# A two-block transformer kernel: latent queries and keys split where they are transposed, a second accumulator bank in the last eight heads, separate banks for the second pair of gates

## The chip, the cores and the metric

The kernel runs on one core of a Trainium2 chip. The metric is the device time of one execution in microseconds (us). Beside the time of each run there is one profiled execution, whose trace tells when each engine did what: PE (TensorE, matmuls; its weight loads are shown apart as PEld), DVE (VectorE), ACT (ScalarE), POOL (GpSimd) and SP (SyncE, which here only issues DMAs).

## The reference, cut to what matters

The input, 1024 tokens of width 1024, goes through two blocks. The first (a mixer of four branches and a gated feed-forward part) is not touched by the change. The second is a hybrid attention layer:

```python
q_a, k_a, v_a, z_a, c_q, c_kv, k_rope, z_b = split(rmsnorm(x) @ w_in)
o_a = dilated_window_attention(rmsnorm(q_a), rmsnorm(k_a), v_a, rel_bias)      # 8 heads of 64
q = rmsnorm(c_q) @ w_uq;  kv = rmsnorm(c_kv) @ w_ukv                          # latent: 8 heads
q_nope, q_rope, k_nope, v = ...            # 64 + 32 wide; norms, then rope on the 32
o_b = softmax(mask((q_nope @ k_nope.T + q_rope @ k_rope.T) * 96 ** -0.5)) @ v
out = x + concat([o_a * silu(z_a), o_b * silu(z_b)]) @ w_out
```

So heads 0 to 7 are windowed heads, and heads 8 to 15 latent heads with queries and keys 96 wide. The gates z_a and z_b are eight blocks ("pairs") of 128 columns.

## The kernel before, in words

Every fp32 matmul is made of matmuls on fp32r operands: a number is split into a high part `hi` (a cast) and a low part `lo` (the number less `hi`), and hi x hi, hi x lo and lo x hi are added up. The helper `split` (lines 99 to 101) does this with a cast on ACT and a subtraction on DVE, or on POOL where it is told so.

The matmul accumulators are eight banks of 128 x 512 fp32: `ip` and `tp` two each, `lt` two, `iq` and `ho` one each. `bank(name)` takes the next free one of a name.

The second block runs in these stages (us from the start of the span):

- About 1760 to 1985: the projections. `compressed`, `latent`, `windowed` and `values` make products of 128 tokens with weights, and their vector work. `latent_out` (line 1600) calls `heads_out` (line 1522) for queries and keys of 128 tokens, and that twice each: PE transposes four heads into the bank `ho`, ACT scales them into a buffer `st` (two of them), and a DMA from ACT's queue stores it in DRAM (`mq`, `mk`, fp32, rows of 512 bytes). There are 8 x 2 x 2 = 32 such calls. `windowed_out` (line 1615) already stores both parts for heads 0 to 7: ACT writes `st`, DVE writes `sl` from the same bank, and two DMAs go out.
- About 1985 to 2015: the gates. `gate_pair` (line 1482) runs 48 matmuls into two banks, then ACT (tanh, line 1498) and DVE (line 1499) empty each. Pair 0 and pair 1 are made here, pairs 2 to 7 (`gates2`) are woven into heads 0 to 7 as filling.
- About 2015 to 2340: the heads. `head_steps` weaves the scores of head h with the value products of head h - 1. A score is two (windowed) or three (latent) matmuls into `lt` or `ho`; DVE adds the mask and takes the minimum (line 1779), ACT takes the exponential (line 1781). The value products (`pv_steps`) go over 12 key blocks, in two groups: 8 blocks for the second half of the queries, then 4 for the first. Per block PE transposes up to four pieces of the probabilities into a bank (line 350), ACT and DVE split that into `pth` and `ptl`, and two matmuls (lines 334 and 335) add to the accumulator `po`. After each group `evict` (line 1801) empties `po`: a copy on ACT (line 1805), a sum on DVE (line 1806); after the second, POOL multiplies with gate and scale (lines 1808 and 1809), and SP stores the result in `mixed`.
- `Head.load` (line 1734) loads a head's queries and keys. For a latent head it loads fp32 `raw` buffers (two) for queries and for keys from `mq` and `mk`, and splits them with a cast on ACT and a subtraction on POOL, 96 x 1024 each. `qh`, `kh`, `kl` and `ql` have two buffers each.
- Beside the latent heads the weights of the output product (`out_weight`, split with POOL) and the first four blocks of `mixed` (`mr`, split with POOL into `mh`, `ml`) are made ready. From about 2320 on the value products of head 15 and the output product follow.

The order on each engine is set by the scheduler of the tile framework, from the program's order and its own estimates; each engine then runs its list in order, and a DMA queue issues in order. So an instruction that waits holds all behind it on its engine.

The lines that decide which bank the heads use:

```python
turns = {"s": ("lt", "lt", "ho"), "pt": ("tp", "tp")}      # line 1721; "pt" are the transposes
banks_ = (lambda: bank("iq"), lambda: next_bank("pt"))     # line 1762; the accumulator is iq
turns["pt"] = ("tp", "tp", "ip", "ip")                     # line 1860, ahead of heads 8 to 15
```

Of the kernel before, what the change touches and what calls it, by code (L numbers as in the profile page):

```python
# [8 lines left out]
F32 = mybir.dt.float32  # L9
F32R = mybir.dt.float32r  # L10
# [55 lines left out]
def kernel(ctx: ExitStack, tc: tile.TileContext, A: dict, out: bass.AP, stop=None):  # L66
# [8 lines left out]
    def f(x):  # L75
        return x.bitcast(F32)
# [1387 lines left out]

    aq_d = dram.tile([2, 512, T], F32, name="aq")
    ak_d = dram.tile([2, 512, T], F32, name="ak")
    mq_d = dram.tile([8, 96, T], F32, name="mq")
    mk_d = dram.tile([8, 96, T], F32, name="mk")
    vt_d = dram.tile([T, 16, 2, 64], F32, name="v2t")
    z_d = dram.tile([1024, T], F32, name="z2")  # L1470
    rd_d = dram.tile([16, T], F32, name="rd")
# [13 lines left out]
    def gate_pair(p, chunks, ps, out):  # L1485

        for half in range(2):
            wh, wl = chunks(0)
            for k in range(4):
                n = 4 * half + k  # L1490
                for w, x, last in ((wh, hh, 0), (wh, hl, 0), (wl, hh, 1)):
                    for j in range(2):
                        PE.matmul(ps[j], w[:, k, :], x[j][:, n, :], start=(n == 0 and w is wh and x is hh),  # L1493
                                  stop=(n == 7 and bool(last)))
                yield
        for j in range(2):
            zt = out()
            S.activation(zt, ps[j], AF.Tanh, scale=0.5)
            V.scalar_tensor_tensor(zt, zt, 1.0, ps[j], op0=ALU.add, op1=ALU.mult)  # L1499
            nc.sync.dma_start(z_d[p * 128:(p + 1) * 128, j * 512:(j + 1) * 512], zt)  # L1500
        yield
# [20 lines left out]
    def heads_out(src, width, dst, t, gain):  # L1522

        for q in range(2):
            pt = quad("ho")[0:width]
            for i in range(4):
                PE.transpose(pt[:, i, :], src[:, 4 * q + i, :], ident)
            st = f(ibw.tile([width, 4, 128], F32R, name="st", bufs=2))
            S.activation(st, pt, AF.Copy, scale=gain)
            S.dma_start(dst[4 * q:4 * q + 4, :, t * 128:(t + 1) * 128].rearrange("h d c -> d h c"), st)  # L1530

    def compressed(t):

# [146 lines left out]
    for p in range(2):  # L1680
        c_ = [gate_weights(p, half, lambda: ibl.tile([128, 512], F32, name="wr", bufs=2).rearrange("p (k c) -> p k c", k=4),
                           lambda: slot(p).rearrange("p (k c) -> p k c", k=4)) for half in range(2)]
        fill.append(gate_pair(p, c_.pop, [bank("ip") for _ in range(2)], lambda: gate_tile()))
        for _ in range(8):
            next(fill[p])
        if p == 0:
            gate_tile = lambda: f(ibw.tile([128, 4, 128], F32R, name="st", bufs=2)).rearrange("p a b -> p (a b)")
            next(fill[p])
# [29 lines left out]
            for _ in range(ZP):  # L1718
                yield

    turns = {"s": ("lt", "lt", "ho"), "pt": ("tp", "tp")}
    turn = {"s": 0, "pt": 0}

    def next_bank(what):
        turn[what] += 1
# [2 lines left out]
    class Head:  # L1728
# [6 lines left out]
        def load(self):  # L1735

            h = self.h
            n = 96 if self.lat else 128
            qh, kh, kl = [at.tile([n, T], F32R, name=name, bufs=2) for name in ("qh", "kh", "kl")]
            if self.lat:  # L1740
                if h == 8:
                    cm_table()
                self.mask = cm[0]
                ql = at.tile([n, T], F32R, name="ql", bufs=2)
                for hi, lo, src in ((qh, ql, mq_d), (kh, kl, mk_d)):
                    raw = at.tile([n, T], F32, name="raw", bufs=2)
                    nc.sync.dma_start(raw, src[h - 8])
                    split(hi, lo, raw, G)
                self.passes = ((qh, kh), (qh, kl), (ql, kh))
            else:  # L1750
                for x, src, ee in ((qh, aq_d, (0, 1)), (kh, ak_d, (0, 0)), (kl, ak_d, (1, 1))):
                    for i, e in enumerate(ee):
                        nc.sync.dma_start(f(x[64 * i:64 * i + 64, :]), src[e, h * 64:(h + 1) * 64, :])
                self.passes = ((qh, kh), (qh, kl))
                self.mask = at.tile([128, T], F32, name="bias", bufs=2)
                nc.sync.dma_start(self.mask, bass.AP(tensor=u_d.tensor, offset=u_d.offset + h * NU, ap=[[1, 128], [1, T]]))

        def values(self):
            h = self.h
            v2 = at.tile([128, 8, 128], F32R, name="v2", bufs=2)  # L1760
            nc.sync.dma_start(f(v2), vt_d[:, h].rearrange("(k p) e d -> p k (e d)", p=128))
            banks_ = (lambda: bank("iq"), lambda: next_bank("pt"))
            self.pv = pv_steps(at, *banks_, v2, self.P, [(1, 0, lambda po: self.evict(po, 1)), (0, 4, lambda po: self.evict(po, 0))],
                               NP_, LAG)
            self.pv.insert(SCL, self.scales)
# [91 lines left out]
    for _ in g2:  # L1857
        pass
    sth.close()
    turns["pt"] = ("tp", "tp", "ip", "ip")  # L1860
    stf = ExitStack()
    fo = stf.enter_context(tc.tile_pool(name="fo", bufs=1, side="right", reuse_waits="tile"))
    for h in range(NG, 16):
# [23 lines left out]
                yield  # L1887

    turns["pt"] = ("tp", "tp")
    braid(weave_steps(heads[15].pv, []), first_products(), FR)  # L1890
    sta.close()
    with tc.tile_pool(name="fp", bufs=1, reuse_waits="tile") as fp:
# [115 lines left out]
```

## Time and profile before

| | |
|---|---|
| median of 3 runs | 2426.95 us (2423.92 to 2432.35) |
| the profiled execution's own time | 2424.3 us |
| its span, first to last instruction | 2422.6 us |
| mean granted clock of TensorE | 0.989 of 2.4 GHz |
| busy: PE, DVE, ACT, POOL | 2322.5, 1467.4, 1067.3, 583.3 us |
| bytes moved by DMA | 309.08 MB |

A stage's table tells for each engine how long it was busy in that stretch; a list of waits tells which engine stood idle until which instruction of another engine ended. The difference between the span and the time, 1.7 us, is what lies around the first and the last instruction.

### The profile page before, as it was taken

To read this page: it belongs to the slowest core of one execution; us is meant where nothing else is said; L and a number is where in the kernel's file an instruction comes from. 1 tells how busy PE (TensorE), PEld (TensorE's weight loads), DVE (VectorE), ACT (ScalarE), POOL (GpSimd) and SP (SyncE) were. 2 spreads that over 40 slices of the span, in tenths; PEclk is the share of its full clock that TensorE was granted. 3 is DMA by queue.
4 is the path that set the end of the run, shared out by engine and by line. 5 is a ranking of instruction groups with operands and counts; after the bars stand their busy time and mean duration, and the time that the engine had idled before them with its cause. 6 is when DMAs were issued, how large, how long until landed. Compare 5 with 4: busy or idle time off the path is not lost.

```text
span 2422.6 us, 31192 instructions
## 1 busy us (share of the span) xinstructions
PE 2322.5 (96%) x11330; PEld 1883.0 (78%) x11330; DVE 1467.4 (61%) x2357; ACT 1067.3 (44%) x1973; POOL 583.3 (24%) x582
## 2 busy tenths in 40 slices
PE   6999899999999999998999997999999999999999
PEld 5887676778777887877788886888798777787787
DVE  4245753578455534579888885556756525678842
ACT  4344433222443323444444342446556525669840
POOL 0122310113223111036555552000023100126510
PEclk9999999999999999999999998999999999999999
DMA  4332115454333258412222224734523647766433
GB/s 153 96 100 83 45 60 165 156 170 138 104 95 105 94 163 240 153 36 79 88 87 81 87 79 152 238 101 150 166 87 109 172 140 206 196 174 186 120 115 134
DMA packets 280442, 309.08 MB, mean 128 GB/s; under 512 B 14928, under 2 KB 209120, under 8 KB 280288
## 3 DMA queue, kind: packets, MB, share of 16 engines
q1 hardware_dynamic: 241296, 266.26, 36.2%
q10 hardware_dynamic: 38848, 40.31, 5.2%
q8 instruction: 89, 1.46, 0.3%
q14 instruction: 65, 0.53, 0.1%
q0 software_dynamic: 144, 0.52, 0.1%
HBM read 217.80 MB, written 89.23 MB: 127 GB/s over the span
## 4 chain that ended last, share of the span: by engine, by line
PE 45%; DMA 5%; DVE 4%; ACT 3%; issue 2%; POOL 1%; SPq 0%; POOLq 0%; ACTq 0%; DVEq 0%
PE ac L1171 11%; PE ip L1171 4%; PE ip L1493 3%; PE tp L350 1%; PE ip L1382 1%; PE ip L1383 1%; PE ip L1384 1%; PE iq L334 1%; PE lt L1777 1%; PE iq L335 1%; DMA wr<-in_w_in_dram 1%; PE ip L1441 1%; PE ip L1043 1%; PE ip L1439 1%; PE ip L1440 1%
## 5 line engine op out<-in xcount | busy, mean ns | idle before, releaser
L123 PE MATMUL mm<-hh,whi 128*128 128x512 f32 x896 | 304.6, 411 | 1.6 <-ACT hh L100 0.9
L123 PE MATMUL mm<-hl,whi 128*128 128x512 f32 x896 | 290.1, 395 | 0.0
L123 PE MATMUL mm<-hh,wlo 128*128 128x512 f32 x896 | 288.4, 393 | 1.3 <-DVE wlo L115 1.3
L100 ACT CAST whi<-wraw 128x1024 fp32r<-128x1024 f32 (+1 forms) x117 | 99.8, 853 | 262.7 <-PE mm L123 197.7
L123 PEld LDWEIGHTS mm<-hh,wlo 128*128 128x128 f32 x896 | 168.6, 189 | 38.8 <-DVE wlo L115 1.9
L123 PEld LDWEIGHTS mm<-hl,whi 128*128 128x128 f32 x896 | 168.1, 189 | 36.0 <-DVE hl L101 0.4
L101 DVE TENSOR_TENSOR wlo<-wraw,whi 128x1024 fp32r<-128x1024 f32 (+1 forms) x117 | 118.2, 1013 | 120.4 <-ACT whi L100 114.6
L123 PEld LDWEIGHTS mm<-hh,whi 128*128 128x128 f32 x896 | 158.9, 190 | 37.7 <-issue 7.1
L167 POOL TENSOR_TENSOR rs<-rs,negh 128x1 f32<-128x1 f32 x32 | 19.5, 612 | 381.1 <-DVE rs L166 381.1
L101 DVE TENSOR_TENSOR gl<-s,gh 128x512 fp32r<-128x512 f32 x88 | 60.7, 690 | 80.3 <-ACT gh L100 77.9
L1781 ACT ACTIVATE p<-p,mn 128x640 f32<-128x640 f32 (+7 forms) x128 | 99.5, 778 | 12.4 <-DVE mn L1779 12.1
L926 POOL TENSOR_TENSOR acc<-acc,pacc 128x1024 f32<-128x1024 f32 x20 | 50.7, 2536 | 199.8 <-DVE acc L921 144.6
L100 ACT CAST uhi<-s 128x1024 fp32r<-128x1024 f32 x42 | 44.1, 1053 | 122.9 <-PE ip L1171 87.6
L101 DVE TENSOR_TENSOR ptl<-tp,pth 128x512 fp32r<-128x512 f32 (+3 forms) x144 | 78.0, 555 | 31.8 <-ACT pth L100 30.6
L100 ACT CAST gh<-s 128x512 fp32r<-128x512 f32 x88 | 54.6, 621 | 94.3 <-PE tp L1440 35.6
L101 DVE TENSOR_TENSOR ulo<-s,uhi 128x1024 fp32r<-128x1024 f32 x42 | 88.0, 2097 | 4.9 <-ACT uhi L100 4.9
L100 ACT CAST pth<-tp 128x512 fp32r<-128x512 f32 (+3 forms) x144 | 66.9, 477 | 43.4 <-PE tp L350 41.3
L1253 POOL TENSOR_TENSOR cv<-th,cv 128x1024 f32<-128x1024 f32 x22 | 53.6, 2434 | 128.6 <-issue 90.2
L334 PE MATMUL iq<-pth,v 128*128 128x512 f32 x192 | 71.7, 375 | 7.8 <-DVE t L1806 4.1
L350 PE MATMUL tp<-cv,p 128*128 128x128 f32 x432 | 71.8, 277 | 1.6 <-DVE ptl L101 1.4
L1808 POOL TENSOR_TENSOR zz<-zz,rdb 128x512 f32<-128x512 f32 x16 | 20.6, 1290 | 216.0 <-DMA qh<-aq 128.2
L1493 PE MATMUL ip<-h3h,zh 128*128 128x512 f32 x192 | 65.6, 409 | 3.7 <-DVE zt L1499 3.7
(591 smaller groups left out, 6437.1 us busy)
## 6 DMA issues: line engine op xcount, KB each, us to landing
wraw<-in_w_in_dram SPq DMA_DIRECT2D x60, 512.0 KB, 4.1
wraw<-in_w_up_dram SPq DMA_DIRECT2D x44, 512.0 KB, 3.9
wr<-in_w_down_dram SPq DMA_DIRECT2D x88, 256.0 KB, 2.9
merged<-acc SPq DMA_DIRECT2D x28, 512.0 KB, 2.9
s<-gg SPq DMA_DIRECT2D x44, 256.0 KB, 4.5
gg<-cv SPq DMA_DIRECT2D x21, 512.0 KB, 2.6
pacc<-merged SPq DMA_DIRECT2D x20, 512.0 KB, 4.1
x<-x ACTq DMA_DIRECT2D x16, 512.0 KB, 2.7
```

The lines of the kernel that those rows point to most:

```text
L100: S.copy(hi, src)
L101: (eng or V).tensor_tensor(lo, src, f(hi), op=ALU.subtract)
L123: PE.matmul(ps[:, c0 + j * 512:c0 + (j + 1) * 512], w[:, k, :], x[j][:, k, :], start=(k == 0 and w is wh and x is xh), stop=(k == nkt - 1 ...
L334: PE.matmul(po[-1][:, w], vh[:, k, :], ph_[:, w], start=(k == 0), stop=False)
L335: PE.matmul(po[-1][:, w], vh[:, k, :], pl_[:, w], start=False, stop=(k == nk - 1))
L350: PE.transpose(pt[:, i * 128:(i + 1) * 128], P[p0 + i][:, k * 128:(k + 1) * 128], ident)
L926: G.tensor_tensor(ac, ac, pa, op=ALU.add)
L1043: PE.matmul(po, ml[:, k, :], W[c][k][0], start=False, stop=(k == NK - 1))
L1171: PE.matmul(acc, a[:, k, :], b[:, k, :], start=(start and k + n == 0), stop=(k == 3 and n == 2), skip_group_check=True)
L1253: G.tensor_tensor(b, self.th, b, op=ALU.mult)
L1493: PE.matmul(ps[j], w[:, k, :], x[j][:, n, :], start=(n == 0 and w is wh and x is hh), stop=(n == 7 and bool(last)))
L1781: S.activation(pr_[:, :L], pr_[:, :L], AF.Exp, scale=-1.0, bias=mn[:, c:c + 1], accum_out=self.den[:, i:i + 1])
```

## The change

1. `heads_out` makes both parts of the latent queries and keys right at the transposes: ACT writes `hi` into `st`, DVE writes `lo` into `sl` from the same bank, and both are stored; `mq` and `mk` get a leading dimension of 2. `Head.load` then loads four tiles, and neither casts nor subtracts. The buffers `raw` are gone.
2. In heads 8 to 15 the accumulator takes turns between `iq` and one of the two `ip` banks, and the transposes rotate over three names in place of four.
3. Gate pair 1 uses `iq` and one `tp` bank; pairs 0 and 2 go on using the two `ip` banks.

```diff
-    mq_d = dram.tile([8, 96, T], F32, name="mq")
-    mk_d = dram.tile([8, 96, T], F32, name="mk")
+    mq_d = dram.tile([2, 8, 96, T], F32, name="mq")
+    mk_d = dram.tile([2, 8, 96, T], F32, name="mk")
...
             pt = quad("ho")[0:width]
             for i in range(4):
                 PE.transpose(pt[:, i, :], src[:, 4 * q + i, :], ident)
-            st = f(ibw.tile([width, 4, 128], F32R, name="st", bufs=2))
-            S.activation(st, pt, AF.Copy, scale=gain)
-            S.dma_start(dst[4 * q:4 * q + 4, :, t * 128:(t + 1) * 128].rearrange("h d c -> d h c"), st)
+            hi = ibw.tile([width, 4, 128], F32R, name="st", bufs=2)
+            lo = ibw.tile([width, 4, 128], F32R, name="sl", bufs=SL)
+            S.activation(hi, pt, AF.Copy, scale=gain)
+            V.scalar_tensor_tensor(lo, pt, gain, f(hi), op0=ALU.mult, op1=ALU.subtract)
+            for e, st in enumerate((hi, lo)):
+                S.dma_start(dst[e, 4 * q:4 * q + 4, :, t * 128:(t + 1) * 128].rearrange("h d c -> d h c"), f(st))
...
-        fill.append(gate_pair(p, c_.pop, [bank("ip") for _ in range(2)], lambda: gate_tile()))
+        fill.append(gate_pair(p, c_.pop, [bank(n) for n in (("ip", "ip"), ("iq", "tp"))[p]], lambda: gate_tile()))
...
-    turns = {"s": ("lt", "lt", "ho"), "pt": ("tp", "tp")}
-    turn = {"s": 0, "pt": 0}
+    turns = {"s": ("lt", "lt", "ho"), "pt": ("tp", "tp"), "po": ("iq",)}
+    turn = {"s": 0, "pt": 0, "po": 0}
...
-                for hi, lo, src in ((qh, ql, mq_d), (kh, kl, mk_d)):
-                    raw = at.tile([n, T], F32, name="raw", bufs=2)
-                    nc.sync.dma_start(raw, src[h - 8])
-                    split(hi, lo, raw, G)
+                for x, src, e in ((qh, mq_d, 0), (kh, mk_d, 0), (kl, mk_d, 1), (ql, mq_d, 1)):
+                    nc.sync.dma_start(f(x), src[e, h - 8])
...
-            banks_ = (lambda: bank("iq"), lambda: next_bank("pt"))
+            banks_ = (lambda: next_bank("po"), lambda: next_bank("pt"))
...
     sth.close()
-    turns["pt"] = ("tp", "tp", "ip", "ip")
+    turns["pt"] = ("tp", "tp", "ip")
+    turns["po"] = ("iq", "ip")
...
     turns["pt"] = ("tp", "tp")
+    turns["po"] = ("iq",)
     braid(weave_steps(heads[15].pv, []), first_products(), FR)
```

The scheduler makes a new order of it. Three places show what moved. Line numbers of the changed kernel are up to 3 higher than those before (the transposes of `windowed_out`, L1618, become L1621; the scores, L1777, become L1778).

The first is PE's list where the latent queries and keys of the later tokens are transposed (`ho<-cv,qq` and `ho<-cv,ko`; `ip` is a projection's bank, `h3h` and `h3l` the parts of the tokens). Before:

```order
L1527 MATMUL ho<-cv,qq 96x128 x4
L1384 MATMUL ip<-s_15266,h3l_11304 128x512
L1382 MATMUL ip<-s_15272,h3h_11302 128x512
L1383 MATMUL ip<-s_15273,h3h_11302 128x512
L1384 MATMUL ip<-s_15272,h3l_11304 128x512
L1382 MATMUL ip<-s_15278,h3h_11302 128x512
L1383 MATMUL ip<-s_15279,h3h_11302 128x512
L1527 MATMUL ho<-cv,ko 96x128 x4
L1384 MATMUL ip<-s_15278,h3l_11304 128x512
```

And after the change:

```order
L1384 MATMUL ip<-s_15344,h3l_11304 128x512
L1527 MATMUL ho<-cv,ko 96x128 x4
L1527 MATMUL ho<-cv,qq 96x128 x4
L1621 MATMUL tp<-cv,an 128x128 x4
L1382 MATMUL ip<-s_15302,h3h_11302 128x512
L1383 MATMUL ip<-s_15303,h3h_11302 128x512
L1384 MATMUL ip<-s_15302,h3l_11304 128x512
L1382 MATMUL ip<-s_15308,h3h_11302 128x512
L1527 MATMUL ho<-cv,qq 96x128 x4
```

Two sets of transposes into `ho` now follow each other with nothing between. A second such pair (`qq`, then `ko`) stands some 55 rows further on, and 26 rows behind that one three sets of `tp<-cv,an` in a row; most other sets stand further apart than before.

The second place is PE's list in a latent head, at the end of its first group of value products. Before:

```order
L334 MATMUL iq<-pth,v_18987 128x128
L335 MATMUL iq<-ptl,v_18987 128x128
L350 MATMUL tp<-cv,p_18999 128x128
L350 MATMUL tp<-cv,p_19017 128x128
L350 MATMUL tp<-cv,p_19033 128x128
L350 MATMUL ip<-cv,p_19017 128x128
L350 MATMUL ip<-cv,p_19033 128x128
L1777 MATMUL lt<-kh,qh 128x256
L1777 MATMUL lt<-kl,qh 128x256
L1777 MATMUL lt<-kh,ql 128x256
```

And after:

```order
L334 MATMUL ip<-pth,v_19067 128x128
L335 MATMUL ip<-ptl,v_19067 128x128
L350 MATMUL tp<-cv,p_19079 128x128
L350 MATMUL tp<-cv,p_19097 128x128
L350 MATMUL tp<-cv,p_19113 128x128
L334 MATMUL iq<-pth,v_19067 128x512
L335 MATMUL iq<-ptl,v_19067 128x512
L350 MATMUL tp<-cv,p_19097 128x128
```

The second group's first products now stand three transposes behind the first group's last, in the other bank; before they stood 22 rows further on, in the same bank.

The third place is SP's list of DMA issues, in one latent head (`raw`, or `qh`, `kh`, `kl`, `ql`, are loads for a later head; `mixed<-t` stores an earlier head; `mr` and `wr` are loads for the output product). Before:

```order
L1761 DMA v_18987<-v2t 128x8x128
L1747 DMA raw<-mq 96x1024
L1747 DMA raw<-mk 96x1024
L1811 DMA mixed<-t_18601 64x512 x2
L1798 DMA zz<-z_13656 64x512 x2
L1838 DMA mr<-mixed 128x1024
L1797 DMA rdb<-rd 64x512 x2
```

And after:

```order
L1830 DMA wr<-in_w_out_dram 128x512
L1839 DMA mr<-mixed 128x1024
L1749 DMA qh<-mq 96x1024
L1749 DMA kh<-mk 96x1024
L1749 DMA kl<-mk 96x1024
L1812 DMA mixed<-t_19183 64x512 x2
L1799 DMA zz<-z_13656 64x512 x2
L1749 DMA ql<-mq 96x1024
L1798 DMA rdb<-rd 64x512 x2
```

Four loads take the place of two; `ql` stands behind the store of an earlier head, the other three ahead of it, behind `mr`.

## Rows read from the trace of the kernel before

**Rows 1.** The page: busy us, share of the span and instructions of each engine.

```profile
PE 2322.5 (96%) x11330; PEld 1883.0 (78%) x11330; DVE 1467.4 (61%) x2357; ACT 1067.3 (44%) x1973; POOL 583.3 (24%) x582
```

**Rows 2.** Table by stage: stretch, length, busy us (count) by engine, clock, DMA.

```profile
core 0: us, PE busy (x) PEld busy (x) DVE busy (x) ACT busy (x) POOL busy (x), PEclk, DMA share, GB/s
...
2015.00:2183.00 168.00, 162.47 (x886) 133.11 (x884) 117.11 (x314) 108.50 (x250) 22.85 (x17) 0.99 0.71 187
2183.00:2320.00 137.00, 127.62 (x773) 106.88 (x772) 110.53 (x313) 121.75 (x279) 73.31 (x42) 0.99 0.50 145
```

**Rows 3.** The same table for the stage that makes latent queries and keys.

```profile
1828.00:1951.00 123.00, 119.62 (x628) 99.01 (x628) 70.76 (x155) 73.59 (x164) 25.14 (x54) 1.00 0.58 161
```

**Rows 4.** Waits of PE, 1990 to 2015: who waited for whom, us, times, longest.

```profile
PE ip L1493 <- DVE zt L1499: 1.2, 1, 1.2
PE ip L1493 <- DVE st L1499: 1.2, 1, 1.2
```

**Rows 5.** Waits, 2183 to 2345, those of PE and its weight loads (PEld).

```profile
PEld iq L334 <- DVE t L1806: 8.5, 12, 1.1
...
PEld iq L334 <- ACT pth L100: 5.3, 7, 1.2
...
PE iq L334 <- DVE t L1806: 4.1, 7, 0.7
...
PE ip L350 <- DVE ptl L101: 2.4, 1, 2.4
PEld iq L335 <- DVE ptl L101: 2.0, 7, 0.4
```

**Rows 6.** Waits of PE's weight loads, 2015 to 2183 (heads 0 to 7).

```profile
PEld tp L350 <- DVE ptl L101: 1.7, 3, 0.7
```

**Rows 7.** Groups of ACT, 2183 to 2320: form, count, busy us, mean ns, idle before.

```profile
L100 ACT CAST qh<-raw 96x1024 fp32r<-96x1024 f32 x7 | 7.4, 1052 | 0.0
L100 ACT CAST kh<-raw 96x1024 fp32r<-96x1024 f32 x7 | 7.3, 1046 | 0.0
...
L100 ACT CAST mh<-mr 128x1024 fp32r<-128x1024 f32 x4 | 4.2, 1050 | 1.8 <-DMA mr<-mixed 1.8
```

**Rows 8.** Groups of POOL, the same stretch.

```profile
L101 POOL TENSOR_TENSOR ql<-raw,qh 96x1024 fp32r<-96x1024 f32 x7 | 16.8, 2401 | 25.6 <-ACT qh L100 25.6
L101 POOL TENSOR_TENSOR kl<-raw,kh 96x1024 fp32r<-96x1024 f32 x7 | 16.8, 2394 | 4.0 <-ACT kh L100 4.0
```

**Rows 9.** The chain that ended last, about 2217 to 2232: start, us, what.

```profile
2217.09 2.40 POOL ql L101
...
2221.79 1.32 POOL t L1809
...
2226.45 3.96 DMA mr<-mixed
2231.38 1.24 ACT p L1781 x2
```

**Rows 10.** Table in slices of 20 us: two whose clock (PEclk) is below 1.00.

```profile
2080.00:2100.00 20.00, 16.97 (x89) 13.79 (x87) 13.19 (x36) 12.16 (x29) 1.29 (x1) 0.91 0.75 198
...
2220.00:2240.00 20.00, 17.04 (x98) 14.79 (x99) 14.55 (x42) 17.03 (x38) 13.20 (x8) 0.91 0.56 168
```

**Rows 11.** Instructions on the tiles `st` and `sl`: duration in ns, least/median/most.

```profile
L1529 ACT ACTIVATE st<-ho,gq x16: 663/686/694, 1833.1 to 1926.2; 96x512 f32<-96x512 f32 x16
...
L1530 ACTq DMA_DIRECT2D mk<-st x16: 311/311/312, 1840.4 to 1931.3; - x16
...
L1622 DVE SCALAR_TENSOR_TENSOR sl<-tp,pv,st x8: 735/745/752, 1769.0 to 1911.7; 128x512 fp32r<-128x512 f32 x8
L1622 DVE SCALAR_TENSOR_TENSOR sl<-tp,gq,st x8: 741/750/752, 1922.0 to 1948.7; 128x512 fp32r<-128x512 f32 x8
```

**Rows 12.** Waits of ACT for landings of stores, 1828 to 1951.

```profile
ACT st L1621 <- DMA aq<-st: 2.8, 2, 2.0
...
ACT st L1529 <- DMA mk<-st: 2.2, 3, 0.8
```

**Rows 13.** Waits of PE, 2015 to 2183.

```profile
PE ip L1493 <- DVE zt L1499: 2.5, 1, 2.5
```

## The prediction

> **What bounds the kernel now.** I read the page's first line for the whole, then the table by stage, then the waits of each stage, and last the chain and the groups of the stage in which the waits are. TensorE is busy for 96% of the span [rows 1], and matmuls are pipelined, so busy does not yet mean full; but it says that a microsecond is won only where TensorE waits, and lost only where it is made to wait. The table by stage shows where that is [rows 2]: in 2015 to 2183 (heads 0 to 7, with gates as filling) PE is busy for 162 of 168 us and ACT and DVE for 108 and 117; in 2183 to 2320 (most of heads 8 to 15, no filling) PE for 128 of 137, ACT for 122 and DVE for 111. So the last eight heads are the stage where three engines stand close together, and there a wait in one is a wait in all. The change works on this stage, on the short stage of the gates ahead of it, and on the stage that writes the latent queries and keys (1828 to 1951), where PE is busy for 120 of 123 us [rows 3].
>
> **Term 1, the gates: -2.4.** Gate pair 1 shared its two banks with pair 0, and pair 2 with pair 1. PE waited twice for the eviction, 1.2 us each [rows 4]. With iq and tp for pair 1 neither wait has a cause: iq and tp have no reader between the last value product and head 0's transposes. The next things that could be late are the weights of pair 2 and the loads of head 0; if these set the pace nothing is won. Bounds 0 and -2.4; I take -2.4, since the order has all of pair 2 that is ready to fill the place.
>
> **Term 2, the second accumulator bank: -7.0.** In 2183 to 2345 the weight loads for the first product of a group waited 12 times, 8.5 us together, for `t L1806`, the DVE half of the eviction that frees iq; the matmul row of the same wait says 4.1 [rows 5]. The changed order puts key group 1 in ip and query group 0 in iq, in turn, so the bank of a group was left a whole group ago. One of the 12 waits belongs to head 15, whose products keep one bank: 8.5 x 11/12 = 7.8 goes. Against it the transposes have three banks for four. Heads 0 to 7 work with two, and there the transposes waited 1.7 us for `ptl` in 168 us [rows 6], 1.4 over 137; halfway between two banks and four that is 0.7 to 0.8. Net -7.0; bounds -4.1 + 1.4 = -2.7 and -8.5.
>
> **Term 3, no splits in the latent heads: -6.2.** ACT loses the casts of qh and kh, 7.4 + 7.3 = 14.7 us in this stage (12% of its 121.75), and POOL the subtractions, 16.8 + 16.8 us [rows 2, 7, 8]. Two things hang on it.
> First, one stall. POOL stood behind `ql` (2.40), so `t` of an earlier head came late (1.32), so its store and the load of mr behind it (3.96 us) did; ACT waited 1.8 us for that with the cast of mh at its head, and behind this cast stood the exp and the `pth` whose `ptl` PE needed [rows 7, 9]. PE lost 2.4 us [rows 5]. In the slice of 20 us that holds the stall the granted clock was 0.91, so part of it ran at 1.2 in place of 2.4 GHz: 9% of 20 us is 1.8 more [rows 10]. With POOL free this chain loses its first two links: -4.2, bounds 0 and -4.2.
> Second, the short waits for ACT: 5.3 us of weight loads for `pth` and 2.0 for `ptl` [rows 5]. In proportion to ACT's work 12% of 7.3, 0.9, would go; all 7.3 at best. DVE keeps all its 111 us, so I stay near the low end: -2.0.
> The new loads (four for two, each of 96x1024) lie on SP's queue ahead of the stores of an earlier head; ql, which has a buffer pair of its own, comes last. qh, kh and kl wait for the buffer of two heads before, so they have one head's time, some 17 us (137 us for eight), to land. I cost them at nothing; the cover is that time.
>
> **Term 4, the price where the parts are made: +5.0.** Each of 32 calls of `heads_out` gains a DVE instruction of the form that `windowed_out` already has, 745 to 750 ns: 32 x 0.745 = 23.8 us, and one more DMA issue on ACT, 32 x 0.31 = 9.9 us of its queue [rows 11]. DVE goes from 70.8 to 94.6 of 123 us, and ACT, 73.6 of 123 plus its issues, stays below the whole [rows 3]. The DMA writes 32 x 197 KB = 6.3 MB more, 51 GB/s over 123 us on top of 161 at a share of 0.58: there is room. So by the sums it is hidden. It shows only where PE returns to the one bank ho too soon: the bank was held for ACT's 0.69 us, and now for 0.69 + 0.75 = 1.43. In the order before, ho's transposes always have other products between them; after, two pairs of them stand back to back, a third pair nearly so, and three groups for the two tp banks follow each other. That is 3 x 1.43 and one wait of about 0.9 for the third tp group, 5.2; I take 5. Bounds: 0 (all hidden, as nearly all is before) and 23.8, if PE met the DVE at every call.
> The trace also shows what the store of a low part does: it stands on ACT's queue behind ACT's own work and waits for the DVE; and the two buffers of `st` already make ACT wait 2.2 and 2.8 us for landings [rows 12].
> The Trainium skill (PSUM — Partial Sum Buffer, section Engine vs sequencer instructions) says that ScalarE's and VectorE's queues are strict first in, first out. By that rule each of the 32 new stores holds ACT for the DVE's 0.745 us and all that stands behind; were it all to reach PE, the sum below would be 18.8 us higher. By the row of the stage [rows 3], in which such stores of `windowed_out` stand too and PE is busy for 120 of 123 us, the sum stands as it is.
>
> **Term 5, the rest: 0.** In heads 0 to 7 no work changes, but the scheduler's order does, because what comes before ends otherwise. This stage has one stall of its own, 2.5 us of PE behind the eviction of a gate pair, and a slice at 0.91 [rows 10, 13]: 2.5 + 1.8 = 4.3 that may vanish, or come twice.
>
> **Sum.** -2.4 - 7.0 - 4.2 - 2.0 + 5.0 = -10.6, against the profiled execution's own 2424.3: 2413.7. That execution lies low among the runs shown (2423.92 to 2432.35), 2.65 under their median of 2426.95. A median of later runs should lie a little above, too; I add half of it, 1.3, and forecast **2415**. A measurement of this kernel can tell about 0.3% from no change, 7.3 us: faster means under 2419.7, slower over 2434.2.
>
> **Rivals.** (a) The stage of the parts becomes bound by the release of ho. Mechanism: transpose, ACT, DVE, next transpose in one bank, with two st and two sl buffers that wait for their stores. Price: 23.8 in place of 5, and today's waits for landings (2.2 + 2.8) once more, 28.8 together: 2424.3 - 15.6 + 28.8 + 1.3 = 2439. It decides from the point where 21 of 32 calls meet the DVE (15.6 / 0.745). For it: the doubled use of two small buffer rings. Against: PE is busy for 120 of 123 us with the same rings today [rows 3], and the order spreads most calls. (b) The last eight heads stay bound: DVE keeps 111 us and now has the largest share after PE, so what `t` no longer costs is waited for at `pth` and `ptl`. Half of term 2, half of the stall, none of the short waits: -2.4 - 3.5 - 2.1 + 5 = -3.0, 2422.6 with the 1.3. For it: three engines within 20 us of each other [rows 2]. (c) The change doesn't do what it says: the loads come behind SP's stores and mr, and each latent head starts about a microsecond late, 8 us that eat term 2: 2423. Against: ql is two heads ahead, the others one. (d) It goes better: the production is hidden (0 for 5), and ACT's relief takes most of the 7.3 (5 more): 2405.
>
> **How the numbers follow.** Forecast 0.45 (its own range 2408 to 2421, which takes in term 5), (a) 0.11, (b) 0.25, (c) 0.07, (d) 0.12. The range from 2404 to 2431 leaves out (a) and the lower half of (d), under 0.2. Faster: nearly all of the forecast (0.42), (d), and a little of (b): 0.57. Slower: (a) and a remnant, 0.12. Between: 0.31.
>
> **What would show it.** After the change: no wait of `ip L1493` for `zt` or `st` ahead of head 0; `iq` and `ip` products of the last eight heads without a wait for `t L1806`, but one at head 15; ACT's stage total down by about 15 us, POOL's by 34; no slice below 1.00 in these heads; the eight heads shorter by 12 to 14 us; in the stage of the parts, waits of `ho` and `tp` transposes for `sl`, about 5 us together. I am wrong if these heads are shorter by less than 6 us, or if PE loses over 12 us more where the parts are made.

## The result, and the profile after

The changed kernel took 2453.41 us in the median of 4 runs (2449.25 to 2459.05), the kernel before 2429.65 us beside it (2423.92 to 2432.47): a ratio of 1.0106, interval 1.0090 to 1.0121. It is slower by about 1.1%, where 0.5% faster was forecast. The profiled execution took 2459.05 us with a span of 2457.3; it lies high among its runs, as that of before lies low, so the two spans differ by 34.7 us, 11 more than the medians.

Where the 34.7 us lie is read from five marks of the trace: the first `ho` transposes of queries, the first matmul of the gates, the first score of head 0, the first product with ql (head 8), the last one (head 15).

| stretch between marks | before | after | |
|---|---|---|---|
| start to the first `ho` transpose (nothing changed there) | 1830.8 | 1834.3 | +3.5 |
| stage of the parts, to the first gate | 154.4 | 180.2 | +25.8 |
| gates alone, to the first score | 30.2 | 30.2 | 0 |
| heads 0 to 7 with gates | 166.7 | 168.6 | +1.9 |
| latent heads, first to last product with ql | 136.2 | 141.2 | +5.0 |
| the rest | 104.3 | 102.8 | -1.5 |

So most of the loss is made where the parts are made, and the eight heads that the change was to shorten became longer. The page's row of busy times after (answers [rows 1]) shows the work itself as forecast: DVE 22 us more, ACT 12 less, POOL 38 less (forecast: 24, 15 and 34).

```profile
PE 2336.6 (95%) x11330; PEld 1890.1 (77%) x11330; DVE 1489.6 (61%) x2389; ACT 1055.7 (43%) x1957; POOL 545.6 (22%) x566
```

The table by stage after, with the columns of [rows 2]: the stage of the parts, the gates, and the latent heads.

```profile
1834.30:2014.50 180.20, 161.59 (x763) 131.17 (x761) 98.20 (x193) 79.45 (x173) 23.28 (x48) 0.94 0.59 168
...
2014.50:2044.70 30.20, 30.20 (x135) 24.98 (x134) 3.96 (x6) 4.69 (x7) 0.00 (x0) 1.00 0.51 144
...
2213.30:2354.50 141.20, 130.52 (x774) 107.30 (x773) 110.97 (x313) 111.33 (x266) 39.85 (x28) 0.99 0.66 183
```

The same stretch of parts before ran 764 matmuls in 151.02 us of PE, at a clock of 1.00 and with 3.4 us idle (154.40 long). Now 763 need 161.59 at 0.94, and 18.6 us are idle. The loss of 25.8 is thus two things of similar size: 15.2 us more in which PE stands, and 10.6 us more that nearly the same matmuls take at a lower mean clock (as an estimate, 6% of 180.2 us is 10.8). Slices of 20 us show where, and two shorter stretches which comes first:

```profile
1854.00:1874.00 20.00, 20.00 (x104) 16.67 (x103) 13.83 (x29) 11.99 (x28) 3.80 (x7) 1.00 0.58 155
1874.00:1894.00 20.00, 16.14 (x79) 12.79 (x77) 14.40 (x33) 11.21 (x27) 4.18 (x7) 0.91 0.69 194
...
1914.00:1934.00 20.00, 14.10 (x74) 10.86 (x73) 13.25 (x27) 11.00 (x25) 6.99 (x14) 0.99 0.68 181
1934.00:1954.00 20.00, 17.28 (x77) 13.87 (x78) 9.84 (x18) 7.28 (x13) 0.00 (x0) 0.84 0.71 188
1954.00:1974.00 20.00, 15.35 (x63) 12.03 (x64) 11.99 (x20) 8.47 (x16) 0.00 (x0) 0.83 0.82 223
1974.00:1994.00 20.00, 20.00 (x93) 16.55 (x92) 5.87 (x9) 5.37 (x9) 0.00 (x0) 1.00 0.44 145
...
1958.00:1968.00 10.00, 5.37 (x29) 4.15 (x27) 5.59 (x9) 4.91 (x9) 0.00 (x0) 0.99 0.90 250
1968.00:1971.00 3.00, 2.99 (x9) 2.54 (x10) 2.35 (x5) 2.07 (x5) 0.00 (x0) 0.50 0.93 265
```

Up to 1874 PE is never idle at 1.00; from there on it stands for 1.5 to 6 us in each slice up to 1974, and the mean clock of the slices falls as far as 0.83; where it no longer stands, it is 1.00 again. 1.00 is 2.4 GHz throughout; the slices at 0.83 and 0.84 hold stretches at the lower level, 1.2 GHz. The standing comes first: from 1958 to 1968 PE stood 4.6 of 10 us at 0.99, and right behind it worked almost without a break at 0.50, which is 1.2 GHz. Nor does the clock of a slice follow its own standing: 1914 to 1934 has the most of it (5.9 us) and still 0.99, and the slice after it 0.84.

What it waits for, from the waits of this stage after (us, times, longest):

```profile
DVE sl L1531 <- ACT st L1530: 33.7, 20, 3.1
...
ACT st L1530 <- PE ho L1527: 11.7, 6, 3.5
...
PE ho L1527 <- DVE sl L1531: 6.3, 4, 2.2
...
PE tp L1621 <- DVE sl L1625: 4.5, 3, 2.1
...
PE tp L1621 <- DVE an L1615: 3.6, 1, 3.6
...
ACT st L1624 <- DMA aq<-st: 3.3, 2, 1.9
```

PE waits for `sl`, as forecast, but for 10.8 us together instead of 5; the next longest of its waits is for `an`, another instruction of DVE (3.6). DVE is not what is slow: it stood 33.7 us waiting for ACT's `st`. And ACT is not full either: it is busy for 79.45 of 180 us, and its 101 DMA issues in this stage (69 before) take another 35.6. Its queue shows why an engine with time to spare is late. Here is a piece of the timeline after (start, length, engine; ACTq are ACT's DMA issues, which do not count as busy):

```profile
1907.09 0.70 ACT L1530 ACTIVATE st<-ho,gq 96x512 fp32r<-96x512 f32 x1
...
1907.82 0.75 DVE L1531 SCALAR_TENSOR_TENSOR sl<-ho,gq,st 96x512 fp32r<-96x512 f32 x1 [3.11 <-ACT st L1530]
...
1908.63 0.31 ACTq L1533 DMA_DIRECT2D mq<-st  x1
...
1909.04 0.44 ACTq L1533 DMA_DIRECT2D mq<-sl  x1
...
1910.07 0.35 ACTq L1580 DMA_DIRECT2D v2t<-vo  x1
...
1910.69 0.67 ACT L1530 ACTIVATE st<-ho,pv 96x512 fp32r<-96x512 f32 x1
```

Between two `st` of ho ACT did 1.9 us of other activations (two casts `vo`, `sq` and a small one) and 1.1 us of issues (0.31, 0.44 and 0.35), in its order. Of the three issues only that of `sl` is new with the change. That reading is a theory until something is taken away. The experiments do that.

### The profile page after: what moved, and what is told of

The parts are those of the page before. It is cut to its first block, busy times and chain, and to the rows that moved or that the text cites. A ratio compares the mean times of both kernels' runs of the same rounds, so it can differ in the third digit from the quotient of the medians.

```text
span 2457.3 us, 31248 instructions
## 1 busy us (share of the span) xinstructions
PE 2336.6 (95%) x11330; PEld 1890.1 (77%) x11330; DVE 1489.6 (61%) x2389; ACT 1055.7 (43%) x1957; POOL 545.6 (22%) x566
## 4 chain that ended last, share of the span: by engine, by line
PE 47%; DMA 4%; DVE 4%; ACT 4%; issue 2%; POOL 1%; SPq 0%; ACTq 0%; POOLq 0%; DVEq 0%
PE ac L1171 11%; PE ip L1171 4%; PE ip L1493 3%; PE ip L1382 1%; PE ip L1383 1%; PE ip L1384 1%; PE tp L350 1%; PE lt L1778 1%; PE ip L1041 1%; PE ip L1040 1%; PE ip L1043 1%; ACT p L1782 1%; PE ip L1441 1%; PE ip L1439 1%; PE ip L1440 1%
## 5 line engine op out<-in xcount | busy, mean ns | idle before, releaser
L123 PEld LDWEIGHTS mm<-hh,wlo 128*128 128x128 f32 x896 | 168.6, 189 | 38.8 <-DVE wlo L115 1.9
L101 DVE TENSOR_TENSOR ptl<-tp,pth 128x512 fp32r<-128x512 f32 (+3 forms) x160 | 86.7, 556 | 36.9 <-ACT pth L100 35.1
L100 ACT CAST pth<-tp 128x512 fp32r<-128x512 f32 (+3 forms) x160 | 74.2, 478 | 51.0 <-PE tp L350 48.8
L350 PE MATMUL tp<-cv,p 128*128 128x128 f32 x481 | 80.6, 276 | 1.9 <-DVE ptl L101 1.4
L1780 DVE CUSTOM_DVE_ANT_0 p<-lt,bias 128x512 f32<-128x512 f32 (+1 forms) x96 | 54.6, 571 | 27.9 <-PE lt L1778 27.3
L350 PEld LDWEIGHTS tp<-cv,p 128*128 128x128 f32 x481 | 58.5, 141 | 13.9 <-PE lt L1778 1.6
```

The costliest lines, as they stand in the source:

```text
L100: S.copy(hi, src)
L101: (eng or V).tensor_tensor(lo, src, f(hi), op=ALU.subtract)
L123: PE.matmul(ps[:, c0 + j * 512:c0 + (j + 1) * 512], w[:, k, :], x[j][:, k, :], start=(k == 0 and w is wh and x is xh), stop=(k == nkt - 1 ...
L350: PE.transpose(pt[:, i * 128:(i + 1) * 128], P[p0 + i][:, k * 128:(k + 1) * 128], ident)
L1780: V.tensor_tensor_reduce(pr_[:, c0:c1], ps[:, 0:c1 - c0], self.mask[:, L - c1:L - c0][:, ::-1], 1.0, mn[:, 0:1] if c else -NEG, ALU.add, A ...
```

## The experiments

Stages are read from one execution of each kernel. How far such a length can be trusted shows where kernels run the same instructions in the stage of the parts: 154.4 us before and in e1, 180.2 after and in e2, 154.6 to 155.3 in the five kernels with the change and all these stores on SP (e6, e11, e12, e14, e17). The stretch ahead of it is less steady, 1825.4 to 1838.1 us in the ten kernels whose edits leave it alone.

**Which of the three changes.** e1 has changes 2 and 3 (both kinds of banks) on the kernel before, e2 has change 1 alone.

> Only the banks of the change (second accumulator bank, own banks for gate pair 1); latent queries and keys are made and split as before. Theory A (the loss of the change is made where the parts are made; in the heads the wait for the eviction only moves to the casts of pth): within 4 us of before, heads 8 to 15 as long as before within 3 us, waits of the products for t gone, waits for pth up. Theory B (the second bank is worth what I forecast): 7 to 10 us faster than before. Theory C (three banks for the transposes cost more than the second accumulator gives): 4 us or more slower than before.

> Only the parts: latent queries and keys split at their transposes, four loads per latent head; banks as before. Theory A: about as slow as the whole change, 20 to 28 us over before, nearly all of it between the first ho transpose and the first gate. Theory C: 12 to 18 us over before, since the banks' share is gone.

e1: 2426.78 us against 2425.25, ratio 1.0007 (0.9995 to 1.0019). e2: 2454.25 us, ratio 1.0120 (1.0102 to 1.0138), its stage of the parts 180.2 us long as with the whole change. The banks are worth nothing that shows, and the whole loss is change 1; the latent heads too are longer in e2 (140.2 us), with the banks of before, and not in e1. Yet the banks did what they say; in the last heads of e1 (2183 to 2346, against [rows 5]):

```profile
PEld ip L334 <- ACT pth L100: 6.8, 10, 1.2
...
PEld iq L334 <- ACT pth L100: 5.0, 13, 0.5
...
PEld iq L334 <- DVE t L1806: 0.3, 1, 0.3
...
PE iq L334 <- DVE t L1806: 0.2, 1, 0.2
```

The wait of the weight loads for `t` fell from 8.5 to 0.3 us, and the one for `pth` rose from 5.3 to 11.8; PE's own wait for `t`, the matmul row, fell from 4.1 to 0.2. The latent heads take 136.2 us in both: PE stands 1.9 us less in them, and its 775 matmuls take 1.9 us more (129.43 against 127.52). In the gates both 1.2 us waits went and 135 instead of 121 matmuls ran ahead of the first score, which came as late as before (30.2 us).

**Which part of change 1.** e3 computes the low parts and does not store them; e4 stores twice and computes none.

```diff
 e3
-            for e, st in enumerate((hi, lo)):
+            for e, st in enumerate((hi,)):
 e4
-            V.scalar_tensor_tensor(lo, pt, gain, f(hi), op0=ALU.mult, op1=ALU.subtract)
-            for e, st in enumerate((hi, lo)):
+            for e, st in enumerate((hi, hi)):
```

> The whole change, but the low parts are computed and not stored: 32 stores fewer, kl and ql are loaded from the high parts, so the scores differ from the reference's. Theory A, in the form that DVE's instruction in the release of ho is what costs: the stage of the parts stays within 6 us of the changed kernel's 180 us. Rival (the stores cost: their issue on ACT, their landing, the two buffers they hold): the stage falls to 155 to 163 us, near the 154 us of before.

> The whole change, but the low parts are not computed: the high part is stored twice, so kl and ql hold the high parts and the scores differ from the reference's. Theory A (DVE in the release of ho): the stage of the parts falls to 155 to 163 us. Rival (the stores): it stays within 6 us of the changed kernel's 180 us. If both kernels fall by half, it is the chain of both.

e3: 2436.15 us, ratio 1.0052 (1.0033 to 1.0071). e4: 2452.72, ratio 1.0116 (1.0097 to 1.0134). The rows of the stage of the parts, e3 and then e4:

```profile
1834.70:1996.30 161.60, 153.69 (x763) 125.40 (x762) 96.98 (x193) 80.42 (x173) 21.47 (x48) 0.99 0.51 149
```

```profile
1834.10:2008.80 174.70, 158.59 (x763) 129.27 (x762) 76.17 (x161) 79.92 (x173) 21.21 (x48) 0.96 0.61 174
```

DVE's instruction without the store costs 7.2 us, the store without DVE's instruction 20.3. The prediction had priced the first and costed the second at nothing. The 20.3 hold more than issues: e4 stores the one buffer `st` twice, and ACT waits there for landings 12.2 us in all, against 6.4 before. Its two longest rows for the stores of `heads_out`:

```profile
ACT st L1622 <- DMA mk<-st: 5.0, 5, 2.2
...
ACT st L1529 <- DMA mq<-st: 4.0, 2, 2.6
```

**What of the store.** Four versions of the whole change: low stores issued by SP (e5), the stores of both helpers issued by SP (e6), one store for both parts in `heads_out` (e8), half the low bytes (e9). The mirror of e5, high stores by SP, is e13.

```diff
 e5
-                S.dma_start(dst[e, 4 * q:4 * q + 4, ...
+                (S, nc.sync)[e].dma_start(dst[e, 4 * q:4 * q + 4, ...
 e6 (in windowed_out too)
+                nc.sync.dma_start(dst[e, 4 * q:4 * q + 4, ...
 e8 (one tile hl in place of st and sl, here and in windowed_out)
+            hl = ibw.tile([width, 2, 4, 128], F32R, name="st", bufs=2)
+            S.dma_start(dst[q, :, :, :, t * 128:(t + 1) * 128].rearrange("e h d c -> d (e h) c"), ...
 e9
+                n_ = (4, 2)[e]
+                S.dma_start(dst[e, 4 * q:4 * q + n_, ...
```

> The whole change, but the 32 stores of the low parts in heads_out are issued by SyncE instead of ScalarE; same bytes, same tiles. Theory I (ScalarE's queue: each store takes it 0.33 us to issue, and the low part's store also waits there for VectorE's 0.75 us, with ScalarE's later work queued behind it): most of what leaving the stores out gave back (17 us) comes back, 2435 to 2441 us. Theory II (the transfers themselves: 6.3 MB more, landings of 4 to 5 us that hold the two buffers of each kind): as the whole change, 2450 to 2457 us. A result between the two would say that both take part. SyncE waiting for the buffer of a gate weight with a store queued behind it could make it slower than 2457.

> The whole change, with all stores of heads_out and windowed_out (64 and 24) issued by SyncE; ScalarE issues only those of the values. Theory I (ScalarE's queue): as low as e5 or lower, 2425 to 2437 us, with ScalarE's starts of st no longer behind an issue. Theory II (the transfers): 2450 to 2457 us.

> The whole change, but high and low part of a call of heads_out lie in one tile and leave in one store of ScalarE: 32 issues instead of 64, the same bytes in the same pieces of 512 bytes; the DRAM tiles are laid out with the two parts of four heads side by side, so that loads of a head are as before. Theory I (ScalarE's queue): 32 issues of 0.33 us go, but the one store still waits for VectorE: about half comes back, 2443 to 2449 us. Theory II (the transfers): the high part now starts 0.75 us later and both buffers come free together: as the whole change or worse, 2450 to 2460 us.

> The whole change, but of each call's four heads only the low parts of the first two are stored (half the bytes, the same number of stores), and the other two heads load a neighbour's low part. Theory I (ScalarE's queue, issue by issue): nothing changes, 2450 to 2457 us. Theory II (bytes or pieces): half of the 17 us comes back, 2443 to 2447 us.

> The mirror of e5: the 32 stores of the high parts in heads_out are issued by SyncE, those of the low parts, which wait for VectorE, stay with ScalarE. If the number of issues on ScalarE counts, as e5: 2438 to 2446 us. If it is the wait for VectorE's low part in ScalarE's order, little comes back: 2449 to 2457 us.

| | issues on ACT in the two helpers, in this stage | us, median | ratio (interval) | stage of the parts, us |
|---|---|---|---|---|
| e9 | 88 | 2452.11 | 1.0098 (1.0081 to 1.0115) | 175.6 |
| e13 | 56 | 2445.52 | 1.0080 (1.0061 to 1.0099) | 166.5 |
| e5 | 56 | 2442.17 | 1.0063 (1.0048 to 1.0078) | 164.2 |
| e6 | 0 | 2431.99 | 1.0023 (1.0013 to 1.0032) | 154.7 |
| e8 | 56 | 2468.89 | 1.0172 (1.0156 to 1.0187) | 191.3 |

Half the low bytes gone took 4.6 us off the stage and 1.3 off the median; the same bytes from another queue took 11 and 21 us off the 2453. The stage of e6 is as long as before (154.4), with all 32 DVE instructions, every byte and the same buffers in it:

```profile
1832.60:1987.30 154.70, 152.50 (x763) 123.32 (x762) 96.68 (x193) 77.54 (x173) 24.27 (x48) 1.00 0.70 196
```

Its waits of the `ho` matmuls for `sl` are 1.7 us where they were 6.3. So DVE's hold on the bank ho, on which term 4 was built, costs little once ACT comes in time: 2 to 4 us, from the five kernels like e6 (154.6 to 155.3) against four without low parts whose stores are on SP too (151.4 to 152.6: e10, e18, e19, e20). e5 and e13 differ by edit only in whether the store left on ACT is the one that waits for DVE there. e13's stage is 2.3 us longer and its median 3.4, but the two intervals overlap, so this part is small and its size not settled.

e8 was expected at 2443 to 2449 by theory I and at 2450 to 2460 by theory II, and is above both, the slowest of all: the count of issues does not set the time alone. In its code the high part's half of the tile is free only when the common store, issued after DVE's part, has landed. The waits of its stage:

```profile
PEld ho L1527 <- DVE st L1530: 12.0, 7, 3.8
PE ho L1527 <- DVE st L1530: 10.2, 7, 3.6
...
ACT st L1529 <- DMA mk<-st: 8.9, 4, 2.8
```

These `st` of ACT now wait 8.9 us for landings of `mk`, against 2.2 before [rows 12], and PE waits 10.2 us for the low half. That the later landing is the whole reason is argued; no run gives e8 more buffers.

**Issues alone.** To the kernel before, without any low part, e16 adds one store of 512 bytes behind each store of `heads_out`.

```diff
+    ju_d = dram.tile([8, 2, 1, 128], F32, name="ju")
...
+            S.dma_start(ju_d[t, q], st[0:1, 0, :])
```

> The kernel before, with 32 more stores on ScalarE's queue of 512 bytes each (one row of st into a DRAM tile that nothing reads), one behind each store of heads_out: no low part, no bytes worth speaking of. Theory I (the number of issues on ScalarE): the stage of the parts grows by 8 to 20 us as it does with the change, 2433 to 2446 us. If the second store costs through its wait for VectorE, its bytes or its buffers: 2424 to 2431 us.

2438.29 us, ratio 1.0061 (1.0038 to 1.0084), inside the range of theory I. The stage of the parts is 15.7 us longer than before; a row of the view of the tile `ju` (least/median/most ns) has the issues:

```profile
1825.40:1995.50 170.10, 159.09 (x764) 130.19 (x762) 76.96 (x161) 80.89 (x173) 20.29 (x48) 0.95 0.49 141
```

```profile
L1532 ACTq DMA_DIRECT2D ju<-st x32: 227/271/474, 1829.1 to 1940.2; - x32
```

32 issues at a median of 0.271 us, about 9 us of ACT's queue, came with 7.6 us more of idle PE (11.0 against 3.4) and, at a clock of 0.95, 8.1 us more of PE work for the same matmuls. No wait in its trace ends with the landing of a `ju`. The reverse, e10, takes the stores of both helpers off ACT in the kernel before:

> The kernel before, with its stores of heads_out and windowed_out (32 and 24) issued by SyncE. If ScalarE's queue is what sets the stage of the parts in any version, the kernel before gains too: 2418 to 2424 us. If it only limits once there are 88 stores in it (before has 56 and its TensorE is busy for 151 of 154 us), nothing: 2424 to 2430 us.

2424.80 us against 2425.34, ratio 0.9991 (0.9978 to 1.0004): nothing that shows, as its second case said, and 1.8 us of the stage:

```profile
1836.20:1988.80 152.60, 151.29 (x764) 124.10 (x763) 75.74 (x161) 77.48 (x173) 25.14 (x48) 1.00 0.54 158
```

With 56 issues and no low part PE hides ACT's queue but for these 1.8 us; with 88, or with 56 and DVE's part behind `st`, it does not.

**The latent heads.** e6 still has the second loss: its latent heads take 141.2 us. It is one stall, in the chain of e6:

```profile
2214.81 7.45 DMA mr<-mixed
...
2222.29 1.03 ACT mh L100
...
2225.86 0.59 ACT pth L100
...
2226.50 0.80 PE ip L334
```

ACT stands at the cast `mh` for a load that took 7.45 us, with `pth` behind it. In the changed kernel itself the same kind of stall hung on `wr` (`DMA wr<-in_w_out_dram`, 8.01 us from 2243.07). e11 moves these casts from ACT to POOL, e12 leaves the loads of the low parts out, e14 gives mr a second buffer.

```diff
 e11
+            G.tensor_copy(mh, mr)
+            G.tensor_tensor(ml, mr, f(mh), op=ALU.subtract)
 e12
-                for x, src, e in ((qh, mq_d, 0), (kh, mk_d, 0), (kl, mk_d, 1), (ql, mq_d, 1)):
+                for x, src, e in ((qh, mq_d, 0), (kh, mk_d, 0)):
...
+                self.passes = ((qh, kh), (qh, kh), (qh, kh))
 e14
-        mr = pool.tile([128, T], F32, name="mr", bufs=1)
+        mr = pool.tile([128, T], F32, name="mr", bufs=MRB)      # MRB = 2
```

> As e6, and the rounded copies of the output weights and of mixed (four foh, four mh) move from ScalarE to GpSimd, which the change has freed. The heads of e6 take 5 us longer than before, all of it at one place, 2222 to 2230 us, where ScalarE waits for mr, which landed 7.45 us after its issue, and the pth behind it. Theory III (that wait on ScalarE): the stall goes, 2425 to 2428 us. Theory IV (the heads are slower for another reason, the transfers or the products): 2430 to 2434 us.

> As e6, but the heads do not load the low parts: kl and ql are left out and the three products of a score all take qh and kh. Loads of the latent heads are back at 0.79 MB each. Theory III, with its cause in the doubled loads: wr and mr land in 3 to 5 us, the stall of 5 us goes, 2425 to 2428 us. If the stall stays (2430 to 2434 us), mr is late for another reason than the loads.

> As e6, with a second buffer for mr, so that the load of one row of mixed need not wait for GpSimd's ml of the one before. Theory V (the order of ScalarE has the casts of mr and wr where the planner takes the loads to have landed, and they land later, with the pth behind): mr is issued up to 5 us earlier and the stall at 2222 to 2230 us shrinks, 2426 to 2430 us, unless the planner moves the cast ahead by as much (then 2430 to 2434). If ScalarE's wait for mr is not what costs the 5 us: 2430 to 2434 us.

e11: 2435.35 us, ratio 1.0035 (1.0024 to 1.0047), worse than e6: the stall at its place went, but POOL now brought `t` later, so SP issued what stands behind its store later, and PE waited in two other heads for the values:

```profile
2240.60 6.68 DMA v<-v2t
...
2264.01 5.94 DMA v<-v2t
```

e12: 2432.62 us, ratio 1.0027 (1.0014 to 1.0040), as e6: the doubled loads are not the cause. In its chain `mr` lands in 4.50 and 3.46 us, sooner than in e6, and nothing is gained by it; the chain runs through POOL (`fol`, `t`, `ml`) and SP's issues instead. e14: 2430.08 us, ratio 1.0017 (1.0004 to 1.0031), its latent heads 138.5 us; half of the 5 us came back in its profiled execution, and its interval overlaps that of e6. To see the heads by themselves, e17 and e18 take the whole work on `wr` and `mr` out of them, in e6 and in e10 (raw tiles from the pool that opens after the last head):

> As e6, but the output weights and the rows of mixed are loaded and split after the last head, and the products that ran beside it follow there: the end is longer by 10 to 25 us and only the stretch of the latent heads is read, from the first to the last product with ql (141.2 us in e6, 136.2 before). Theory V (casts of mr and wr on ScalarE are the loss): 132 to 136 us, below e18. If the heads of the change are slower in themselves (four loads, products): 138 to 142 us, above e18.

> The same edit on e10 (the kernel before with its stores on SyncE): the stretch from the first to the last product with ql was 135.3 us there. Without the casts of mr and wr the splits of qh, kh, ql and kl remain on ScalarE and GpSimd: 133 to 136 us. Theory V puts it above e17 by 1 to 4 us; the other way, below e17 by 4 us or more.

The latent heads of e17 and then of e18:

```profile
2189.00:2325.20 136.20, 129.34 (x775) 106.30 (x773) 111.30 (x313) 103.35 (x254) 20.45 (x16) 1.00 0.59 158
```

```profile
2184.50:2318.70 134.20, 125.03 (x775) 105.92 (x774) 109.64 (x311) 114.79 (x263) 53.62 (x30) 1.00 0.41 117
```

The work on `wr` and `mr` costs the change 5.0 us (141.2 in e6 to 136.2) and the kernel before 1.1 (135.3 in e10 to 134.2). So 3.9 of the 5.9 us between e6 and e10 come from there. But theory V had put e17 below e18 and it is 2 us above: without any of this, with 11 us less of ACT and 33 less of POOL, the heads of the change are not faster. One execution each, and the two differ in the banks too (e19 below, with the banks of the change and the splits of before, has 136.2 against the 135.3 of e10); that the heads are slower in themselves is not settled.

**The pieces together.** e19 is the kernel before with the banks of e1 and the stores of e10; e20 adds the second buffer for mr.

> The best of the parts so far, without latent parts from the transposes on: the kernel before with the banks of e1 and the stores of e10. Its pieces by the profiles: the stage of the parts 152.6 us (154.4 before), heads 0 to 7 158.7 us (160.6 before). If these add, 2420 to 2423 us; if each was only how one execution fell, 2424 to 2428 us.

> As e19, with the second buffer for mr of e14, which gave e6 2.7 us in its latent heads. Before, the same stretch lost only 1.1 us to the casts (e10 against e18), so at most 1 us more than e19: 2419 to 2423 us if the pieces add, 2424 to 2428 us if not.

e19: 2423.41 us against 2426.39, ratio 0.9993 (0.9983 to 1.0003). e20: 2422.60, ratio 0.9981 (0.9970 to 0.9992): below both kernels, by 0.2%, less than the 0.3% that the prediction called faster. Neither holds low parts in DRAM.

## Why the prediction was wrong

**Term 4 failed, and with it the sign.** It forecast +5.0 and the stage measured +25.8. That is 20.8 of the 38 us between 2415 and 2453; the gains of terms 1 to 3, 15.6 us, did not come either, and the latent heads lost 5.0 instead. The step was "ACT, 73.6 of 123 plus its issues, stays below the whole", with the conclusion "So by the sums it is hidden". The sums were right (DVE's 0.75 us, an issue of 0.31 us) and did not matter: what PE returns to is not a stage total but the next `st` in ACT's order, and each issue put into that order shifts all `st` behind it. e16 shows it with issues alone (+15.7), e4 with stores without DVE's part (+20.3, waits for landings in it), and e6 takes it away with everything else left in (+0.3). The other half of the step, the hold of the bank ho by DVE, was the part priced; it costs 7.2 us where 56 issues are on ACT (e3) and 2 to 4 where none are. "There is room" for the bytes held in the main: e6 moves all of them in a stage as long as before.

Term 4 also had no price for the clock, though terms 3 and 5 had one for a slice at 0.91. Of the 25.8 us the longer matmuls make 10.6.

The rule of the Trainium skill that the text weighed (PSUM — Partial Sum Buffer, section Engine vs sequencer instructions: in-order queues of ScalarE) spoke against the change, and I set it aside because the row of the stage was full. It would have given 2434, nearer than 2415. What it was applied to, ACT standing for DVE's 0.75 us, is the smaller part here: 2.3 us of the stage between e5 and e13. By the same order each issue holds what stands behind it, and that is the larger part (15.7 us in e16).

**Rival (a)** had the right stage and nearly its price (28.8 against 25.8; its 2439 falls short because it kept the gains of terms 1 to 3), by a mechanism that is the smaller part: release of ho and full buffer rings. e6, with the same rings and the same release, is 0.3 us above before. ACT's waits for landings of these stores were 6.4 us before, 9.3 after and 3.9 in e6, not doubled as the rival had them. In e4 (12.2) and e8 the rings do matter, where one buffer has to serve both stores or one store both parts.

**Term 1 (-2.4)**: both waits went, and nothing came of it where it was looked for; the first score is as late as before after the first gate. In e1 the gates' matmuls done early are missing from heads 0 to 7 (830 against 843), and this stretch is 1.9 us shorter (158.7 against 160.6); the whole stays within its interval, so a gain of about a microsecond is neither shown nor excluded.

**Term 2 (-7.0)**: the waits for `t` went, 8.5 to 0.3 us, and the time did not (136.2 us, e1). Rival (b) had named it: with DVE at 111 us, what `t` no longer costs is waited for at `pth`. The failed steps were to take the 8.5 us of the weight loads, which overlap the matmuls, where PE itself had stood 4.1 for `t` [rows 5], and to subtract the wait as if nothing were behind it.

**Term 3 (-6.2)**: ACT and POOL lost the work as forecast; after, 111.33 and 39.85 us in these heads. The stall [rows 9] did not go; it came back at another link of the same chain, a cast on ACT waiting for `mr` or `wr`. The step "With POOL free this chain loses its first two links" took the order on ACT as given. It changed, as the instructions of ACT in its order show for the second group of casts (before, then after; the number is the place in ACT's order):

```
1513 L100 CAST foh_19043<-wr 128x512
1515 L100 CAST foh_19291<-wr 128x512
1532 L100 CAST mh_19297<-mr 128x1024

1553 L100 CAST foh_19367<-wr 128x512
1554 L100 CAST mh_19373<-mr 128x1024
1555 L100 CAST foh_19617<-wr 128x512
```

`mh` stood 17 places behind a `foh` and now stands between two of them. The trace agrees: these three casts started at 2210.53, 2211.41 and 2222.17 us before, and at 2248.44, 2249.96 and 2251.11 after. In the third group before, where the stall of [rows 9] lies, `mh` already stood two places behind a `foh`; so the order alone does not tell where a stall falls. That the planner put it there because POOL looked free is argued, not shown. The share of DMA time in these heads rose from 0.50 to 0.66, but e12, at 0.54, is no faster than e6, so this is not what the 5 us are made of.

**Term 5 (0)**: heads 0 to 7 took 1.9 us more, inside what the text allowed for.

What stays open: how much of the price of an issue is its own time on ACT and how much the other order that the planner makes once the issue is in it (no kernel here holds the order fixed); why e8 is as slow as it is; and the last 2 us between e17 and e18.

## What to carry to other kernels

A DMA issued from an engine that also evicts banks is work of that engine: count its issues, and ask which eviction stands behind each one, even where the busy share of the engine is half. If another queue is idle, move the issues before adding to them; here that alone was worth 21 us to the changed kernel and nothing that shows to the one before. A wait taken from the engine that is busy all the time pays only if the next thing it needs is already there, as `pth` was not in e1: look for what is second latest, and expect a wait removed in one place to turn up there.

## What was unexpected on the chip

- Stores of 512 bytes cost three quarters of what stores of 197 KB did: 32 of them, 0.27 us each, made the stage 15.7 us longer (e16); in e4 32 of 197 KB made it 20.3 longer.
- Where the parts are made PE stood 15.2 us more after the change, and its matmuls took 10.6 us more at a granted clock of 0.94: the lower clock cost two thirds as much again. The mean clock of this stage goes with its length: 1.00 in the eleven kernels here at 151.4 to 155.3 us, 0.99 at 161.6 and 164.2, 0.98 at 166.5, 0.95 and 0.96 from 170.1 to 175.6, 0.94 at 180.2, 0.92 at 191.3.
- The load of 512 KB `mr` landed in 3.96 us in the stall before [rows 9] and in 7.45 us in that of e6.
